# q, k, v projections with the weights stationary, and transposes back to token rows, in a hybrid decoder layer

## The chip, the cores and the metric

The kernel runs on one core of one Trainium2 chip. A core has a matrix engine (TensorE; the profile calls its matmuls PE and its weight loads PEld), a vector engine (VectorE, DVE), a scalar engine (ScalarE, ACT), a general one (GpSimd, POOL) and a queue engine that only starts transfers (SyncE, SP). The metric is the device time of one execution in microseconds, as the median of three runs.

## The reference, cut to what matters

One layer of a decoder runs for 1024 prompt tokens and 64 sample tokens, 1088 in all, of 1024 features, in float32. The part that matters here sits between the two feed-forward blocks:

```
h = rms(x)
[q | k | v | u | g_a | g_b] = h @ w_in      # q, k, v: 768 features each = 12 heads x 64
q = head_rmsnorm(q);  k = head_rmsnorm(k)   # mean of squares over the 64 features of a head
A = dilated sliding-window attention, 3 groups of 4 heads, (window, dilation) =
    (128, 1), (512, 4), (2048, 16)
B = causal pooling over u
x += (sigmoid(g_a) * (A @ w_attn_branch) + sigmoid(g_b) * (B @ w_pool_branch)) @ w_out
```

The normed k and the raw v of the last tokens are outputs too.

## The kernel before, in words

Every float32 product is made of three matmuls on a high and a low part (`mm3`, lines 252 to 259): high by high, high by low, low by high. The normed activations lie in SBUF as `h_hi` and `h_lo`, features on partitions, 8 blocks of 128 features by 1088 tokens. The tokens are cut into three chunks `CH` of 364, 362 and 362 columns (line 30).

`proj` (line 261) multiplies a 128-wide piece of a weight (stationary) by a chunk of tokens (moving): 24 matmuls, with 128 features on the partitions of the result. The feed-forward blocks, the pooling input u and the gates g_a and g_b go this way.

q, k and v go another way, in `qkv` (line 644), called for head group 2, then 1, then 0, each time for q, k and v ("kinds") of 256 features. For the dilated groups the prompt tokens are needed in another order: group 2 takes every eighth token into one tile of 128, group 1 every fourth. `permuted` (line 599) picks such a tile straight from `h_hi` and `h_lo`, with a step of 8 or 4 elements, as the stationary operand; the 256 columns of the weight move. The result has tokens on partitions. A ninth tile holds tokens 960 to 1087, of which only the last 64, the sample tokens, are used. Five units a kind (four of two tiles, one of the ninth) each fill one PSUM bank of the pool "a" (`psa`, four banks). For q and k the unit then goes through `qk_norm` (line 707): ScalarE squares it, VectorE sums over each head, makes the inverse root in eleven small steps and multiplies; for k GpSimd multiplies by the gain; TensorE transposes the rows back to features on partitions (line 737), and ScalarE copies them to `qT` or `kT`. For v a copy to `vs` is all.

The order of the work is written out by an `Interleaver` (line 72): a clock counts microseconds of TensorE work as the dense matmuls are emitted, and jobs (the head norms, attention of the group before, `sample_scores` with its loads every 2.7 us of that clock, the pooling) are let in when the clock reaches their due time. A scheduler of the language then orders each engine's instructions from that. Scores, transposes and values of attention use the other four PSUM banks, pool "b" (`psb`). After the last group come the eight gate projections; while they run, the second half of the sample attention and the combination of the groups are done, and the merge waits for both.

Of the kernel before, what the change touches and what calls it, by code (L numbers as in the profile page):

```python
# [29 lines left out]
CH = ((0, 364), (364, 362), (726, 362))  # L30
# [87 lines left out]
def body(ctx, tc, x_prompt, x_sample, c128, c512, c2048, state_pool, rel_bias_table,  # L118
# [27 lines left out]
    def tmp():  # L146
        return tmp_pool[0].tile([P, 364], F32, tag="tmp", name="tmp", bufs=8)
# [130 lines left out]
    def rsqrt(v, y, t):  # L278
        """y = v ** -0.5: exponent-halving seed, then three Newton steps."""
# [38 lines left out]
    def normed(xt, c, gi, dg):  # L318
        """h = x * gain * r for a chunk, r on the diagonal blocks of dg."""
# [100 lines left out]
    def biases():  # L420
        """The bias of every lag, in the order that the layouts of the score tiles read them."""
# [21 lines left out]
    for c, (c0, n) in enumerate(CH):  # L443
# [22 lines left out]
        dg = ip.tile([P, 364], F32, tag="dg", name="dg", bufs=2)[:, :n]  # L466
# [16 lines left out]
    # sample rows' biases: 128 cached positions, then the 64 new tokens  # L483
# [62 lines left out]
    def pooling():  # L546
# [22 lines left out]
        for gi in range(4):  # L569
# [22 lines left out]
            for c0, n in CH:  # L592
                o = psb()[:, :n]
                PE.matmul(o, wgr[:, gi, :], d[:, c0:c0 + n], start=True, stop=True)
                y = pp.tile([P, 364], F32, tag="y", name="y", bufs=2)[:, :n]
# [3 lines left out]
    def permuted(g, t):  # L599
        """AP picker over h tiles for the 128 tokens of permuted tile t of group g."""  # L600
        if t == 8:
            return lambda a, k: a[:, k, TP - NS:T]
        if g == 0:
            return lambda a, k: a[:, k, t * P:(t + 1) * P]
        if g == 1:
            c, hf = t // 2, t % 2
            return lambda a, k: a[:, k, c + 512 * hf:c + 512 * hf + 509:4]
        return lambda a, k: a[:, k, t:t + 1017:8]

    def token_rows(dst, g, t):  # L610
        """Rows of dst (indexed by token) that tile t of group g holds."""
# [7 lines left out]
    def reversed_rows(dst, g, t):  # L619
        """Rows of dst (indexed by the token counted from the end) of tile t's reversed tokens."""  # L620
# [7 lines left out]
    def store_kv(g, t, kind, tl):  # L628
        if t == 8:
            G.dma_start(out=kv_scr[kind, g], in_=tl[NS:P, :])  # L630
# [13 lines left out]
    def qkv(g, gp, follow):  # L644
        qT = gp.tile([P, 2, TP], F32, name="qT")
        kT = gp.tile([P, 2, TP], F32, name="kT")
        vs = [gp.tile([P, 256], F32, name=f"v{t}") for t in range(8)]
# [3 lines left out]
        for kind in range(3):  # L651
            c0 = kind * AW + g * 256
            w = taken()
            if kind < 2:
# [4 lines left out]
                if kind == 0:  # L659
                    V.tensor_scalar(out=gt, in0=gt, scalar1=0.125, scalar2=None, op0=ALU.mult)  # L660
            for u in range(5):
                if u == 1:
                    fetch(wi[:, c0 + AW:c0 + AW + 256] if kind < 2 else follow)
                tiles = (2 * u, 2 * u + 1) if u < 4 else (8,)
                nt = len(tiles)
# [6 lines left out]
                if kind == 2:  # L672
                    for i, t in enumerate(tiles):
                        if t < 8:
                            vt = vs[t]
                        else:
                            vt = qp.tile([P, 256], F32, tag="v8", name="v8", bufs=1)
                        S.activation(vt, o[:, i * 256:(i + 1) * 256], AF.Copy)
                        store_kv(g, t, 1, vt)
                    il.advance(0.325)  # L680
                    continue
                jobs.append(il.spawn(qk_norm(g, kind, tiles, o, gt, qT if kind == 0 else kT,
                                             qs if kind == 0 else ks)))
                il.advance(0.325)
# [12 lines left out]
        for job in jobs[:5]:  # L697
            il.finish(job)

# [5 lines left out]
        return qT, kT, vs, il.spawn(tail(), 6)  # L705

    def qk_norm(g, kind, tiles, o, gt, dst, dst8):
# [3 lines left out]
        sq = xq()  # L711
        S.activation(sq[:, :n], o[:, :n], AF.Square)
        st = qp.tile([P, 3, 8], F32, tag="st", name="st", bufs=3)
        v, y, t_ = st[:, 0, :nh], st[:, 1, :nh], st[:, 2, :nh]
# [4 lines left out]
        xn = xq()  # L719
        V.tensor_tensor(out=xn[:, :n].rearrange("p (h d) -> p h d", d=64),  # L720
                        in0=o[:, :n].rearrange("p (h d) -> p h d", d=64),
                        in1=y.unsqueeze(2).to_broadcast([P, nh, 64]), op=ALU.mult)
        xv = xn[:, :n].rearrange("p (t f) -> p t f", f=256)
        if kind == 1 or nt == 1:
            G.tensor_tensor(out=xv, in0=xv, in1=gt.unsqueeze(1).to_broadcast([P, nt, 256]),
                            op=ALU.mult)
        for i, t in enumerate(tiles):
            if kind == 1:
                store_kv(g, t, 0, xn[:, i * 256:(i + 1) * 256])
            elif t == 8:  # L730
                G.dma_start(out=q_scr[g], in_=xn[NS:P, 0:256])
                q_ready[g] = True
        yield 5.5
        tr = psb()
        for i in range(nt):
            for hp_ in range(2):
                PE.transpose(out=tr[:, (hp_ * nt + i) * P:(hp_ * nt + i + 1) * P],
                             in_=xn[:, i * 256 + hp_ * P:i * 256 + (hp_ + 1) * P],
                             identity=flip if kind == 0 and nt == 2 else ident)
# [7 lines left out]
        else:  # L747
            S.activation(dst8, tr[:, :256].rearrange("p (a x) -> p a x", a=2)[:, :, NS:], AF.Copy)

    def attention(g, qkvs):  # L750
# [47 lines left out]
        def values(t, kt, us, pts):  # L798
            o = psb()[:, :256]
            for h in range(4):  # L800
                for i, k in enumerate(kt):
                    PE.matmul(o[:, h * 64:(h + 1) * 64], pts[i][:, h * P:(h + 1) * P],  # L802
                              vs[k][:, h * 64:(h + 1) * 64], start=i == 0, stop=i == len(kt) - 1)
# [19 lines left out]
    def sample_scores():  # L823
        """Products of each sample query with its cached keys, keys on partitions."""
# [187 lines left out]
    ctx_a, ctx_b = ExitStack(), ExitStack()  # L1012
    ga_p = ctx_a.enter_context(tc.tile_pool(name="ga_p", bufs=1))
# [28 lines left out]
    def second_half():  # L1042
# [4 lines left out]
        ctx_a.close()  # L1047
        cp = cmctx.enter_context(tc.tile_pool(name="cmb", bufs=2))
# [5 lines left out]
    def merge_inputs():  # L1054
        """The pooled and attended branches, split for the products of the merge."""
        for c0, n in CH:
            for i in range(6):
                t = y_p.tile([P, 364], F32, tag="yl", name="yl", bufs=3)[:, :n]
# [55 lines left out]
    # merge, output projection  # L1114
# [121 lines left out]
```

## Time and profile before

| | |
|---|---|
| median of three runs | 2544.18 us (2540.89 to 2544.44) |
| span of the profiled execution, first to last instruction | 2539.3 us |
| the profiled execution's own time beside that | not given; the span is 4.9 us under the median |
| mean granted TensorE clock | 0.994 |
| PE busy / PEld busy / DVE busy / ACT busy / POOL busy | 2511.2 / 2468.5 / 1146.0 / 583.5 / 200.3 us |

The busy time of an engine is the time in which at least one of its instructions was under way. Matmuls overlap one another in the records, so what one of them costs is read from the distance between the starts of neighbours and not from the length of its record. The stages of q, k and v follow one another: group 2 from 878.5 to 1037.0 us, group 1 to 1199.6 us, group 0 to 1313.1 us, and then the gates to about 1566 us.

### The profile page before, as it was taken

The page shows a single profiled execution, that of the slowest core. Times are in us where ns is not written, and L with a number is a line of the kernel's source. Part 1 is how long each engine was busy: PE and PEld are TensorE (multiplying, and loading weights), DVE is VectorE, ACT ScalarE, POOL GpSimd, SP SyncE. Part 2 cuts the span into 40 slices and gives each one's busy share as a digit, 9 for nine tenths or more (in the row PEclk, how much of TensorE's full clock was granted, in tenths as well). Part 3 has the DMA queues.
Part 4 walks back from the last instruction along what each step waited for, and adds up shares of the span by engine and source line. Part 5 has one row for each costly group of instructions (what it writes and reads, how often), then busy time and mean ns, then how long its engine had stood idle before and what let it go on. Part 6 is the DMA issues. An engine that isn't in the chain of part 4 may idle for free. (4 is left out here: it accounts for less than half of the span.)

```text
span 2539.3 us, 36519 instructions
## 1 busy us (share of the span) xinstructions
PE 2511.2 (99%) x15192; PEld 2468.5 (97%) x15192; DVE 1146.0 (45%) x2451; ACT 583.5 (23%) x1233; POOL 200.3 (8%) x317
## 2 busy tenths in 40 slices
PE   7999999999999999999999999999999999999999
PEld 6999999999999999999989979999999999999998
DVE  6333343333336634255887723737333334433334
ACT  5211111111112312132334213214111111111111
POOL 4200000000001202012021211002000000000001
PEclk8999999999999999999999999999999999999999
DMA  4311221212221211235574685541122222221132
GB/s 140 103 58 42 83 83 66 83 47 70 83 83 64 69 34 70 84 122 161 170 236 141 205 288 181 176 177 34 50 83 83 75 76 83 77 73 67 42 116 71
DMA packets 153591, 257.24 MB, mean 101 GB/s; under 512 B 12581, under 2 KB 122853, under 8 KB 152641
## 3 DMA queue, kind: packets, MB, share of 16 engines
q1 hardware_dynamic: 141296, 224.26, 26.8%
q0 software_dynamic: 12128, 30.64, 3.6%
q8 instruction: 119, 1.95, 0.3%
q14 instruction: 48, 0.39, 0.0%
HBM read 225.99 MB, written 73.57 MB: 118 GB/s over the span
## 5 line engine op out<-in xcount | busy, mean ns | idle before, releaser
L257 PE MATMUL psa<-h_hi,wh 128*128 128x362 f32 (+1 forms) x2784 | 916.6, 330 | 2.4 <-ACT h_hi L328 2.2
L258 PE MATMUL psa<-h_lo,wh 128*128 128x362 f32 (+1 forms) x2784 | 915.0, 329 | 1.8 <-DVE h_lo L329 1.8
L259 PE MATMUL psa<-h_hi,wl 128*128 128x362 f32 (+1 forms) x2784 | 916.5, 329 | 0.0
L357 DVE SCALAR_TENSOR_TENSOR xt<-psb,xt 128x364 f32<-128x364 f32 (+1 forms) x528 | 279.7, 534 | 635.4 <-PE psb L259 635.1
L257 PEld LDWEIGHTS psa<-h_hi,wh 128*128 128x128 f32 x2784 | 525.4, 189 | 12.3 <-issue 7.2
L258 PEld LDWEIGHTS psa<-h_lo,wh 128*128 128x128 f32 x2784 | 527.0, 189 | 4.7 <-DVE h_lo L329 2.1
L259 PEld LDWEIGHTS psa<-h_hi,wl 128*128 128x128 f32 x2784 | 525.5, 189 | 1.4 <-issue 0.8
L257 PE MATMUL psb<-hh,dh 128*128 128x362 f32 (+1 forms) x1056 | 347.6, 329 | 0.0
L258 PE MATMUL psb<-hl,dh 128*128 128x362 f32 (+1 forms) x1056 | 346.7, 328 | 0.0
L259 PE MATMUL psb<-hh,dl 128*128 128x362 f32 (+1 forms) x1056 | 346.1, 328 | 0.0
L257 PE MATMUL psa<-wh,h_hi 128*128 128x256 f32 x648 | 231.2, 357 | 0.0
L258 PE MATMUL psa<-wl,h_hi 128*128 128x256 f32 x648 | 230.3, 355 | 0.0
L259 PE MATMUL psa<-wh,h_lo 128*128 128x256 f32 x648 | 229.6, 354 | 0.0
L213 DVE TENSOR_TENSOR wl<-wr,wh 128x1024 fp32r<-128x1024 f32 (+1 forms) x142 | 168.2, 1206 | 86.8 <-ACT wh L212 86.8
L257 PEld LDWEIGHTS psb<-hh,dh 128*128 128x128 f32 x1056 | 198.7, 188 | 0.2
L259 PEld LDWEIGHTS psb<-hh,dl 128*128 128x128 f32 x1056 | 198.8, 188 | 0.0
L258 PEld LDWEIGHTS psb<-hl,dh 128*128 128x128 f32 x1056 | 198.7, 188 | 0.1
L212 ACT ACTIVATE dh<-dr 128x256 fp32r<-128x256 f32 x176 | 72.2, 417 | 504.1 <-PE psb L258 494.9
L212 ACT ACTIVATE wh<-wr 128x1024 fp32r<-128x1024 f32 (+1 forms) x142 | 141.1, 1040 | 181.3 <-PE psa L258 163.5
L258 PEld LDWEIGHTS psa<-wl,h_hi 128*128 128x128 f32 x648 | 178.4, 275 | 1.6 <-issue 1.0
L257 PEld LDWEIGHTS psa<-wh,h_hi 128*128 128x128 f32 x648 | 178.2, 275 | 1.2 <-issue 0.3
L259 PEld LDWEIGHTS psa<-wh,h_lo 128*128 128x128 f32 x648 | 178.5, 275 | 0.5 <-issue 0.3
(225 smaller groups left out, 1913.2 us busy)
## 6 DMA issues: line engine op xcount, KB each, us to landing
wr<-in_ffn_w_up_dram SPq DMA_DIRECT2D x88, 512.0 KB, 4.0
out_dram<-in_cache_kv_w_dram SPq DMA_DIRECT2D x32, 1020.0 KB, 8.8
qb<-q_scr SPq DMA_DIRECT2D x96, 256.0 KB, 4.0
dr<-in_ffn_w_down_dram SPq DMA_DIRECT2D x44, 512.0 KB, 4.4
wr<-in_w_in_dram SPq DMA_DIRECT2D x38, 512.0 KB, 4.6
kt<-in_cache_kv_w_dram SPq DMA_DIRECT2D x64, 256.0 KB, 3.8
vt<-in_cache_kv_w_dram SPq DMA_DIRECT2D x26, 512.0 KB, 8.0
t<-t_scr SPq DMA_DIRECT2D x16, 544.0 KB, 5.2
```

Of the source, the lines that this page charges most:

```text
L212: S.activation(hi, src, AF.Copy)
L213: V.tensor_tensor(out=lo, in0=src, in1=hi.bitcast(F32), op=ALU.subtract)
L257: PE.matmul(out, lh, rh, start=i == 0, stop=False)
L258: PE.matmul(out, lh, rl, start=False, stop=False)
L259: PE.matmul(out, ll, rh, start=False, stop=i == n - 1)
L357: V.scalar_tensor_tensor(out=xd, in0=o, scalar=0.5, in1=xd, op0=ALU.mult, op1=ALU.add)
```

## The change

The chunks become 360, 360 and 368 columns, so that all their borders are multiples of 8, and the temporaries that hold a chunk grow to 368. q, k and v are projected by `proj`, as u and the gates are: weights stationary, features on the partitions, six calls a kind. ScalarE copies each result out of PSUM into a tile `raw` and permutes the tokens as it does (`permute`), reading PSUM with a step of 8 or 4 elements. `token_major` then transposes each token tile back to token rows on TensorE, into a bank of pool "b", and the head norm reads that bank as it read the projection's bank before. The five norm jobs of a kind are let in from 1.5 us of the clock after the kind's last projection, 2 us apart, instead of one after each unit. The eight value tiles become one. The ninth tile has the 64 sample tokens alone. GpSimd's scratch for transfer descriptors is set to 4096 bytes instead of its default. Comments are blanked.

```diff
-CH = ((0, 364), (364, 362), (726, 362))
+CH = ((0, 360), (360, 360), (720, 368))
...
-    def permuted(g, t):
-        if t == 8:
-            return lambda a, k: a[:, k, TP - NS:T]
         if g == 0:
-            return lambda a, k: a[:, k, t * P:(t + 1) * P]
-        if g == 1:
-            c, hf = t // 2, t % 2
-            return lambda a, k: a[:, k, c + 512 * hf:c + 512 * hf + 509:4]
-        return lambda a, k: a[:, k, t:t + 1017:8]
+    def permute(g, dst, o, c):
+        c0, n = CH[c]
+        m = min(n, TP - c0)
+        if g == 0:
+            S.activation(dst[:, c0:c0 + n], o, AF.Copy)
+            return
+        if g == 2:
+            S.activation(dst[:, :TP].rearrange("p (r i) -> p r i", r=8)[:, :, c0 // 8:(c0 + m) // 8],
+                         o[:, :m].rearrange("p (i r) -> p r i", r=8), AF.Copy)
+        else:
+            dv = dst[:, :TP].rearrange("p (r f i) -> p r f i", r=4, f=2)
+            for hf in range(2):
+                a, b = max(c0, 512 * hf), min(c0 + m, 512 * hf + 512)
+                if a < b:
+                    S.activation(dv[:, :, hf, (a - 512 * hf) // 4:(b - 512 * hf) // 4],
+                                 o[:, a - c0:b - c0].rearrange("p (i r) -> p r i", r=4), AF.Copy)
+        if m < n:
+            S.activation(dst[:, TP:], o[:, m:n], AF.Copy)
...
     def qkv(g, gp, follow):
+            raw = [rp.tile([P, T], F32, tag="raw", name="raw") for _ in range(2)]
...
+            for f in range(2):
+                for c in range(3):
+                    if f == 0 and c == 1:
+                        fetch(wi[:, c0 + AW:c0 + AW + 256] if kind < 2 else follow)
+                    o = proj(w, f, c, h_hi, h_lo)
+                    permute(g, raw[f], o, c)
+                    go()
             for u in range(5):
-                if u == 1:
-                    fetch(wi[:, c0 + AW:c0 + AW + 256] if kind < 2 else follow)
                 tiles = (2 * u, 2 * u + 1) if u < 4 else (8,)
-                o = psa()
-                for i, t in enumerate(tiles):
-                    pk = permuted(g, t)
-                    mm3(o[:, i * 256:(i + 1) * 256],
-                        [(pk(h_hi, k), pk(h_lo, k), w[0][:, k, :], w[1][:, k, :])
-                         for k in range(KD)], 0.325)
...
-                jobs.append(il.spawn(qk_norm(g, kind, tiles, o, gt, qT if kind == 0 else kT,
-                                             qs if kind == 0 else ks)))
-                il.advance(0.325)
+                jobs.append(il.spawn(
+                    values_of(g, tiles, raw, vs) if kind == 2 else
+                    qk_norm(g, kind, tiles, raw, gt, qT if kind == 0 else kT,
+                            qs if kind == 0 else ks), 1.5 + 2 * u))
...
+    def token_major(raw, tiles):
+        o = psb()
+        rows = P if len(tiles) == 2 else NS
+        for i, t in enumerate(tiles):
+            for a in range(2):
+                PE.transpose(out=o[:rows, i * 256 + a * P:i * 256 + (a + 1) * P],
+                             in_=raw[a][:, t * P:t * P + rows], identity=ident)
+        return o[:rows, :len(tiles) * 256]
...
+    rp = rctx.enter_context(tc.tile_pool(name="rp", bufs=3))
...
-    nc = bacc.Bacc("TRN2", target_bir_lowering=False, num_devices=1)
+    nc = bacc.Bacc("TRN2", target_bir_lowering=False, num_devices=1,
+                   dynamic_dma_scratch_size=4096)
```

## Rows read from the trace of the kernel before

**Rows 1.** The page's first part: busy us (share of the span) xinstructions.
```profile
PE 2511.2 (99%) x15192; PEld 2468.5 (97%) x15192; DVE 1146.0 (45%) x2451; ACT 583.5 (23%) x1233; POOL 200.3 (8%) x317
```

**Rows 2.** Windows by stage: length, busy us of each engine (count), clock, DMA share, GB/s.
```profile
878.50:1037.00 158.50, 158.50 (x712) 156.13 (x711) 54.93 (x174) 27.76 (x54) 27.16 (x43) 1.00 0.20 63
1037.00:1199.60 162.60, 162.60 (x836) 160.77 (x836) 83.33 (x235) 40.81 (x118) 20.96 (x29) 1.00 0.40 128
1199.60:1313.10 113.50, 111.29 (x925) 106.99 (x925) 91.10 (x243) 41.48 (x121) 17.47 (x24) 1.00 0.56 177
1313.10:1566.00 252.90, 248.20 (x1691) 224.19 (x1690) 131.87 (x260) 73.62 (x182) 40.27 (x69) 0.99 0.66 216
```

**Rows 3.** Timeline of PE in group 2: start us, length, instruction.
```profile
899.79 0.40 PE L257 MATMUL psa<-wh,h_hi 128*128 128x256 f32 x1
...
911.14 0.41 PE L259 MATMUL psa<-wh,h_lo 128*128 128x256 f32 x1
911.39 0.60 PE L737 MATMUL psb<-flip,xq 128*128 128x128 f32 x4
911.74 0.49 PE L257 MATMUL psa<-wh,h_hi 128*128 128x256 f32 x1
912.07 0.41 PE L258 MATMUL psa<-wl,h_hi 128*128 128x256 f32 x1
```

**Rows 4.** The same in group 1 and, from 1199.64, in group 0.
```profile
1188.43 0.40 PE L257 MATMUL psa<-wh,h_hi 128*128 128x256 f32 x1
...
1199.40 0.39 PE L259 MATMUL psa<-wh,h_lo 128*128 128x256 f32 x1
1199.64 0.28 PE L257 MATMUL psa<-wh,h_hi 128*128 128x256 f32 x1
...
1209.58 0.28 PE L259 MATMUL psa<-wh,h_lo 128*128 128x256 f32 x1
```

**Rows 5.** Timeline of PEld in group 2, at the border of the ninth tile.
```profile
1034.54 0.34 PEld L259 LDWEIGHTS psa<-wh,h_lo 128*128 128x128 f32 x1
1034.78 0.21 PEld L257 LDWEIGHTS psa<-wh,h_hi 128*128 128x128 f32 x1
1034.92 0.19 PEld L258 LDWEIGHTS psa<-wl,h_hi 128*128 128x128 f32 x1
...
1037.66 0.31 PEld L257 LDWEIGHTS psa<-wh,h_hi 128*128 128x128 f32 x1
```

**Rows 6.** Timeline of PE in the projection of u, weights stationary.
```profile
871.73 0.32 PE L257 MATMUL psa<-h_hi,wh 128*128 128x362 f32 x1
...
878.43 0.33 PE L259 MATMUL psa<-h_hi,wl 128*128 128x362 f32 x1
```

**Rows 7.** Groups by shape: busy us, mean ns | idle before; ACT and DVE copies from PSUM.
```profile
L1103 ACT ACTIVATE xq<-psa 128x362 f32<-128x362 f32 x32 | 14.9, 464 | 54.8 <-PE psa L259 50.1 <-issue 4.8
L1188 DVE COPY yo<-psa 128x256 f32<-128x256 f32 x8 | 3.4, 420 | 1.4 <-issue 0.8 <-PE psa L1181 0.6
```

**Rows 8.** The strided copies out of PSUM in the sample attention (tile pz).
```profile
L946 DVE COPY pz<-psb x1: 425/425/425, 1446.6 to 1446.6; 128x256 f32<-128x256 f32 x1
```

**Rows 9.** Timeline of the head norm of one q unit, ACT and DVE.
```profile
902.89 0.60 ACT L712 ACTIVATE xq<-psa 128x512 f32<-128x512 f32 x1 [7.38 <-PE psa L259]
903.52 0.69 DVE L715 TENSOR_REDUCE st<-xq 128x8 f32<-128x512 f32 x1 [4.08 <-ACT xq L712]
...
906.72 0.69 DVE L720 TENSOR_TENSOR xq<-psa,st 128x512 f32<-128x512 f32 x1
```

**Rows 10.** Groups of POOL from 878 to 1313 us: busy us, mean ns | idle before.
```profile
L725 POOL TENSOR_TENSOR xq<-xq,gt 128x512 f32<-128x512 f32 (+1 forms) x18 | 21.7, 1204 | 65.8 <-DVE xq L720 38.4 <-issue 16.6 <-PE psb L737 10.8
```

**Rows 11.** Groups of DVE in group 1's stage, 1037 to 1200 us.
```profile
L827 DVE TENSOR_TENSOR qb<-kt,qb 128x512 f32<-128x512 f32 x27 | 19.5, 722 | 6.6 <-DMA qb<-q_scr 6.6
L829 DVE TENSOR_REDUCE sc<-qb 128x8 f32<-128x512 f32 x27 | 18.4, 683 | 0.3
```

**Rows 12.** All products of the sample scores: duration ns min/median/max, first and last start.
```profile
L827 DVE TENSOR_TENSOR qb<-kt,qb x96: 670/684/1657, 1040.5 to 1427.5; 128x512 f32<-128x512 f32 x96
```

**Rows 13.** DMA issues: KB each, median us to landing.
```profile
qb<-q_scr SPq DMA_DIRECT2D x96, 256.0 KB, 4.0
x_scr<-xt POOLq DMA_DIRECT2D x2, 1448.0 KB, 7.3
```

More of the change, by code (lines that the diff above doesn't have):

```diff
@@ L146, in tmp @@
     def tmp():
-        return tmp_pool[0].tile([P, 364], F32, tag="tmp", name="tmp", bufs=8)
+        return tmp_pool[0].tile([P, 368], F32, tag="tmp", name="tmp", bufs=8)
     ident = const.tile([P, P], F32, name="ident")
@@ L465, in body @@
         rsqrt(st[:, 0, ts], st[:, 1, ts], st[:, 2, ts])
-        dg = ip.tile([P, 364], F32, tag="dg", name="dg", bufs=2)[:, :n]
+        dg = ip.tile([P, 368], F32, tag="dg", name="dg", bufs=2)[:, :n]
         t0 = c0
@@ L629, in store_kv @@
         if t == 8:
-            G.dma_start(out=kv_scr[kind, g], in_=tl[NS:P, :])
+            G.dma_start(out=kv_scr[kind, g], in_=tl[:NS, :])
             G.dma_start(out=kvs[g][:, WIN[g] - Q:WIN[g], kind * 256:(kind + 1) * 256],
@@ L646, in qkv @@
         kT = gp.tile([P, 2, TP], F32, name="kT")
-        vs = [gp.tile([P, 256], F32, name=f"v{t}") for t in range(8)]
+        vs = gp.tile([P, 8, 256], F32, name="vs")
         jobs = []
@@ L703, in tail, with values_of, qk_norm @@
             yield from new_scores()
-        return qT, kT, vs, il.spawn(tail(), 6)
-    def qk_norm(g, kind, tiles, o, gt, dst, dst8):
+        return qT, kT, vs, il.spawn(tail(), 11)
+    def token_major(raw, tiles):
[6 more added lines that the diff above has]
+        return o[:rows, :len(tiles) * 256]
+    def values_of(g, tiles, raw, vs):
+        o = token_major(raw, tiles)
+        il.clock += 0.22 * len(tiles)
+        if len(tiles) == 1:
+            vt = xq()[:, :256]
+            S.activation(vt[:NS], o, AF.Copy)
+            store_kv(g, 8, 1, vt)
+            return
+        S.activation(vs[:, tiles[0]:tiles[0] + 2, :], o.rearrange("p (t f) -> p t f", f=256), AF.Copy)
+        for t in tiles:
+            store_kv(g, t, 1, vs[:, t, :])
+        return
+        yield
+    def qk_norm(g, kind, tiles, raw, gt, dst, dst8):
         nt = len(tiles)
@@ L710, in qk_norm @@
         nh = nt * 4
-        sq = xq()
-        S.activation(sq[:, :n], o[:, :n], AF.Square)
+        o = token_major(raw, tiles)
+        rows = o.shape[0]
+        il.clock += 0.22 * nt
+        sq = xq()[:rows]
+        S.activation(sq[:, :n], o, AF.Square)
         st = qp.tile([P, 3, 8], F32, tag="st", name="st", bufs=3)
-        v, y, t_ = st[:, 0, :nh], st[:, 1, :nh], st[:, 2, :nh]
+        v, y, t_ = st[:rows, 0, :nh], st[:rows, 1, :nh], st[:rows, 2, :nh]
         V.tensor_reduce(out=v, in_=sq[:, :n].rearrange("p (h d) -> p h d", d=64), axis=AX.X,
@@ L718, in qk_norm @@
         rsqrt(v, y, t_)
-        xn = xq()
+        xn = xq()[:rows]
         V.tensor_tensor(out=xn[:, :n].rearrange("p (h d) -> p h d", d=64),
-                        in0=o[:, :n].rearrange("p (h d) -> p h d", d=64),
-                        in1=y.unsqueeze(2).to_broadcast([P, nh, 64]), op=ALU.mult)
+                        in0=o.rearrange("p (h d) -> p h d", d=64),
+                        in1=y.unsqueeze(2).to_broadcast([rows, nh, 64]), op=ALU.mult)
         xv = xn[:, :n].rearrange("p (t f) -> p t f", f=256)
         if kind == 1 or nt == 1:
-            G.tensor_tensor(out=xv, in0=xv, in1=gt.unsqueeze(1).to_broadcast([P, nt, 256]),
+            G.tensor_tensor(out=xv, in0=xv, in1=gt[:rows].unsqueeze(1).to_broadcast([rows, nt, 256]),
                             op=ALU.mult)
@@ L730, in qk_norm @@
             elif t == 8:
-                G.dma_start(out=q_scr[g], in_=xn[NS:P, 0:256])
+                G.dma_start(out=q_scr[g], in_=xn[:, 0:256])
                 q_ready[g] = True
@@ L736, in qk_norm @@
             for hp_ in range(2):
-                PE.transpose(out=tr[:, (hp_ * nt + i) * P:(hp_ * nt + i + 1) * P],
-                             in_=xn[:, i * 256 + hp_ * P:i * 256 + (hp_ + 1) * P],
-                             identity=flip if kind == 0 and nt == 2 else ident)
+                x = xn[:, i * 256 + hp_ * P:i * 256 + (hp_ + 1) * P]
+                if nt == 1:
+                    PE.transpose(out=tr[:, hp_ * NS:(hp_ + 1) * NS], in_=x,
+                                 identity=ident[:NS, :NS])
+                else:
+                    PE.transpose(out=tr[:, (hp_ * nt + i) * P:(hp_ * nt + i + 1) * P], in_=x,
+                                 identity=flip if kind == 0 else ident)
+        il.clock += 0.22 * nt
         if nt == 2 and kind == 0:
```

24 lines of the change are left out of this document (7 added, 17 removed).

## The prediction
> **What bounds the kernel now.** I read the page's busy times first. TensorE is busy 99% of the span and its weight loads 97%, with no other engine above 45% [rows 1], so whatever shortens TensorE's stream shortens the kernel until another engine or a transfer comes to be late. The busy share doesn't say what a matmul costs, so next come the windows by stage: groups 2, 1 and 0 take 158.5, 162.6 and 113.5 us, 434.6 us in all, at a granted clock of 1.00, with 2.2 us of idle PE, all of it in group 0 [rows 2]. The three issue the same dense matmuls, 1944 in all (3 groups, 3 kinds, 9 tiles, 24 each). The timeline tells why they differ. In group 2, 48 matmuls from 899.79 to 911.14 are 47 distances of 0.2415 us [rows 3]; in group 1, 47 distances from 1188.43 to 1199.40 are 0.2334; in group 0, 83 distances from 1199.64 to 1209.58 are 0.1198 [rows 4]. The moving operand is 256 contiguous columns in all of them; only the step of the stationary tile differs: 8, 4 and 1. The ninth tile, which is contiguous in every group, is the control: at its border, inside group 2, the weight load falls from 0.34 to 0.19 us and 24 loads take 2.88 us, 0.12 each [rows 5]. So groups 2 and 1 are bound by strided weight loads.
>
> **What the projections cost before.** A kind has 8 strided tiles of 24 matmuls and one contiguous. Group 2: 576 x 0.2415 + 72 x 0.1198 = 147.7 us. Group 1: 576 x 0.2334 + 72 x 0.1198 = 143.1. Group 0: 648 x 0.1198 = 77.6. Sum 368.4 us. The other 66.2 us of the stages are transposes, pooling products, attention of the group before and the idle time; they stay.
>
> **What they cost after.** Six calls of 24 matmuls a kind, 1296 in all, on 1088 / 3 = 362.7 columns on average. The same form, weights stationary and contiguous, ran in the projection of u: 42 matmuls of 362 columns, 41 distances from 871.73 to 878.43, 0.1634 us each [rows 6]; scaled to 362.7 columns 0.1637, so 212.2 us. The rows of the ninth tile that were computed twice are gone in this.
>
> **Transposes added.** Per kind 8 tiles x 2 and 2 for the sample rows, 162 in all. Four in group 2 lie between the matmuls that start at 911.14 and 912.07; less two distances of 0.24 that is 0.45 us for four, 0.112 each with the slower restart behind them [rows 3]. 162 x 0.112 = 18.1 us. The transposes back exist already. Net: 368.4 - 212.2 - 18.1 = 138.1 us off TensorE's stream. The chunks of 360 and 368 move the same columns everywhere else: nothing.
>
> **ScalarE's permuting copies.** About 63 of them, less the value copies that go. The nearest copy is 0.464 us for 362 columns [rows 7]; below I bound a strided one at that, above at twice. All but the last of a kind are hidden by the dense matmuls behind them (four banks in pool "a", 24 matmuls or 3.9 us each). The last one stands before the first transposes, which come 1.5 us of clock later, so it needs no wait at 0.5 us; at 0.9 us with a weight split ahead on ScalarE, 9 waits of at most 1 us. In group 1's window ScalarE goes from 40.8 us in 162.6 to some 52 in 96. I take 0 to 9 us and put 2 into the sum.
>
> That a step in PSUM is free, the trace shows for VectorE: 256 columns read with a step of 64 took 425 ns against 420 contiguous [rows 7, 8]. The Trainium skill (Advanced Engine Details and Errata, PSUM Cachelines) asks that every two consecutive PSUM elements be contiguous for best throughput, and `permute` reads with steps of 4 and 8. By the rule the copies are at their upper bound and the sum 7 us worse; by the row it stays. The skill's SBUF page (SBUF — State Buffer, Door 1) calls a step of up to 4 float32 free; by that group 1 would have run like group 0 and the gain would be 65 us smaller, which the 0.2334 contradicts.
>
> **Head norms, the one place where work is bunched.** The chain of a unit runs from 902.89 to 907.41, 4.5 us, of which VectorE holds 3.9 [rows 9]; k adds 1.2 us on GpSimd [rows 10]. Before, units came 5.2 us of clock apart; now five come 2 us apart behind a kind. Queued behind them on VectorE are the weight splits and the sample products, and each unit now holds a bank of pool "b" for some 6 us, which attention wants too. TensorE itself needs nothing from the chain but the transposes back: until then it has the next kind's dense matmuls, 3.9 us a call, about 23 us in all. The limit is VectorE's total. In group 1 it was busy 83.3 us of 162.6 [rows 2]; the stage shrinks to 162.6 - 143.1 + 70.7 + 6.0 = 96.2 us. The sample products (1.4 us a pair) follow the clock, which is as long as before and slightly more, so 27 pairs become some 29 [rows 11]: 86 us, plus some 4 us of gaps between the small steps. Group 0: 91.1 + 7 us in 113.5 - 77.6 + 70.7 + 6.0 = 112.6, less the idle time. Group 2, without sample products, 54.9 in 87.5. So VectorE is 94% full in group 1 and 87% in group 0. Below, nothing is lost; above, if every wait for a sample load (6.6 us in group 1 [rows 11]) and the bunching show, some 25 us. Group 0 ran at 80% before and lost 2.2 us [rows 2], the nearest row; I take 6.
>
> **Transfers.** Group 1 moved 128 GB/s at a share of 0.40 [rows 2], which is 0.68 in 96.2 us; the gates ran at 0.66 with 216 GB/s, so the queues have carried it. The next weights are fetched after one call of six instead of one unit of five, 18 us before use against a landing time near 5. The stores of k and v go out on POOL in the same number, later by up to a kind; nothing waits for them before the second half of the sample attention. The smaller descriptor scratch touches POOL's queue: if its 1448 KB spills blocked POOL for their 7.3 us [rows 13], only the last of three would have little cover; 0 to 7 us, and I take 0, since 24 matmuls of the u projection, four times over, stand before each norm's result.
>
> **Sum.** The span of 2539.3 lies 4.9 under the median of 2544.2, and I take that margin as fixed. 2539.3 - 138.1 + 2 + 6 = 2409.2 in span, 2414 us in time.
>
> **Rivals.** *VectorE becomes the bound in groups 1 and 0:* its queue holds back the transposes, pool "b" stays full and TensorE idles for the 25 us above: 2433 us. For it speaks the 94%; against it that the work can slide into group 2's end and the gates, where VectorE is half idle [rows 2].
>
> *The sample attention becomes late:* its 96 products span 1040.5 to 1427.5, 4.0 us each [rows 12], while the clock asks for 2.7. If loads and not the clock set that pace, they still need 387 us, and the second half 136 us more (1430 to 1566), 523 us from group 1's start; TensorE would have 96 + 113 + 253 = 462. The merge then waits 61 us: 2475 us. Against it: group 2's step of 0.24 where the clock counted 0.108 explains the pace, and a load lands in 4.0 us [rows 13].
>
> *Every chain lies bare:* the banks of pool "b" are so taken that TensorE stops at each unit until its norm is through. 12 pairs of q at 4.5 us, 12 of k at 5.7, 6 ninth tiles at 3.8 and 9 last copies at 1 us make 154 us, more than the 138 saved: 2560 us, slower. It turns slower once nine tenths of that price are paid, that is, if the next kind's dense matmuls cover almost nothing.
>
> *The change doesn't do what it says:* the slow weight load isn't the step's doing, or the strided copies stall pool "a" as much. The ninth tile in the same group speaks against it; half the gain would be left, 2475 us.
>
> **Chances.** Forecast 0.74 (own range 2400 to 2424), VectorE the bound 0.13, sample late 0.06, half the gain 0.04, chains bare 0.03. The range of 2398 to 2440 takes in the first two and leaves out 0.13; its low end is the sum with no stall and with the idle time of group 0 and some of the gates' 4.7 us [rows 2] gone. All but the last are faster by over 0.2%, the 5 us that a measurement of this kernel can tell: faster 0.96, same 0.01, slower 0.03.
>
> **What would show it.** PE distances of 0.163 us on 360 columns in all three stages, no PEld of 0.33 us left, stages near 88, 96 and 113 us; 162 more transposes at about 0.11; PE idle under 10 us from group 2 to the merge. Wrong it is if PE sits idle before the transposes on VectorE or ScalarE, if VectorE shows over 95% in group 1 with PE waiting, or if the gates' stage grows beyond 253 us.

## The result and the profile after

The changed kernel takes 2478.87 us (median of 4 runs, 2476.85 to 2484.49), the one before 2544.31 beside it: a ratio of 0.9751, 95% interval 0.9737 to 0.9764. So 65 us came of the 130 that the prediction has, and the time lies 39 us above the upper end of its range. The profiled run took 2478.45 us with a span of 2476.7. Its page, first part, answers to [rows 1]:

```profile
PE 2400.4 (97%) x14706; PEld 2344.0 (95%) x14706; DVE 1151.3 (46%) x2451; ACT 604.0 (24%) x1293; POOL 203.2 (8%) x317
```

TensorE now idles for 76.3 us of the span, 28.1 before. Windows by stage, the borders put where the dense matmuls of one group end and the next begin; columns and stages as in [rows 2] (groups 2, 1, 0, gates):

```profile
876.76:962.38 85.62, 85.62 (x517) 81.83 (x517) 42.89 (x126) 28.14 (x58) 13.29 (x22) 1.00 0.25 76
962.38:1056.89 94.51, 93.62 (x615) 89.71 (x615) 61.22 (x177) 40.97 (x120) 20.43 (x30) 1.00 0.51 160
1056.89:1205.03 148.14, 122.75 (x740) 112.44 (x739) 100.33 (x258) 49.52 (x137) 22.24 (x31) 0.86 0.54 169
1205.03:1507.84 302.81, 273.57 (x1830) 245.84 (x1830) 162.48 (x354) 88.14 (x225) 53.34 (x83) 0.93 0.61 197
```

Groups 2 and 1 are done in 85.6 and 94.5 us, as forecast (88 and 96). Group 0 takes 148.1 instead of 113 and the gates, counted here up to the first matmul of the merge, 302.8 instead of 253 (257.3 by that border before). From the merge on nothing changed: 968.9 us to the end in both. The clock of the third column from the right says that the two bad stages also ran part of the time at half speed.

The dense matmuls themselves are what was forecast. PE's timeline in group 2, answering to [rows 3, 4], and the groups of ScalarE's permuting copies by shape (busy us, mean ns | idle before), answering to [rows 7]:

```profile
890.73 0.33 PE L258 MATMUL psa<-h_lo,wh 128*128 128x360 f32 x1
...
896.95 0.33 PE L257 MATMUL psa<-h_hi,wh 128*128 128x360 f32 x1
```

```profile
L607 ACT ACTIVATE raw<-psa 128x360 f32<-128x360 f32 x12 | 5.6, 475 | 22.3 <-PE psa L259 16.0 <-PE psb L710 4.5 <-issue 1.7
L604 ACT ACTIVATE raw<-psa 128x360 f32<-128x360 f32 x12 | 5.4, 473 | 8.3 <-PE psa L259 7.2 <-PE psb L710 1.0
L614 ACT ACTIVATE raw<-psa 128x360 f32<-128x360 f32 x6 | 2.9, 487 | 3.9 <-PE psa L259 3.8
```

38 distances in 6.22 us are 0.1637 us each, the number of the sum. L607 reads PSUM with a step of 8, L614 with a step of 4, L604 contiguously: 475, 487 and 473 ns.

What was not forecast are the holes in TensorE. Its two longest sums of waits in the whole run (waited for: us in total, times, longest):

```profile
PE psb L766 <- POOL xq L749: 35.1, 6, 12.1
PE psb L817 <- ACT s L808: 6.3, 4, 2.5
```

L766 are the transposes of a normed unit back to columns, L749 is the k gain on GpSimd, the last step of the norm chain. One of the deepest holes lies at 1063 to 1093 us, at the k units of group 1 (a "unit" is a pair of token tiles, or the ninth, on its way through the head norm). First PE, start us, length, instruction, and in brackets the idle time before it:

```profile
1062.75 0.33 PE L259 MATMUL psa<-h_hi,wl 128*128 128x360 f32 x1
...
1074.36 3.62 PE L710 MATMUL psb<-ident,raw 128*128 128x128 f32 x16
1087.41 1.12 PE L766 MATMUL psb<-ident,xq 128*128 128x128 f32 x4 [9.43 <-POOL xq L749]
1089.21 0.64 PE L710 MATMUL psb<-ident,raw 128*64 128x128 f32 x2 [0.69 <-ACT kT L774]
1090.19 0.67 PE L257 MATMUL psa<-h_hi,wh 128*128 128x360 f32 x1 [0.35 <-ACT raw L614]
1090.66 0.50 PE L258 MATMUL psa<-h_lo,wh 128*128 128x360 f32 x1
...
1093.06 0.37 PE L257 MATMUL psa<-h_hi,wh 128*128 128x360 f32 x1
```

The last dense matmul is at 1062.75; then come only attention of group 2, the first transposes of four units (L710), a wait, the first unit's transposes back and, behind them, the first transposes of the fifth unit (128*64, at 1089.21). VectorE in the same stretch; L856 and L858 are a sample product and its sum, L739 and L744 the first and last step of a unit's norm:

```profile
1074.16 0.69 DVE L856 TENSOR_TENSOR qb<-kt,qb 128x512 f32<-128x512 f32 x1 [3.20 <-DMA qb<-q_scr]
...
1080.06 0.69 DVE L856 TENSOR_TENSOR qb<-kt,qb 128x512 f32<-128x512 f32 x1 [1.09 <-DMA qb<-q_scr]
1080.67 0.68 DVE L739 TENSOR_REDUCE st<-xq 128x8 f32<-128x512 f32 x1
...
1085.32 0.69 DVE L744 TENSOR_TENSOR xq<-psb,st 128x512 f32<-128x512 f32 x1
```

The first unit's square was ready at 1076.1; VectorE takes it up at 1080.67, behind products that wait for their loads. And ScalarE:

```profile
1075.46 0.60 ACT L736 ACTIVATE xq<-psb 128x512 f32<-128x512 f32 x1 [0.47 <-PE psb L710]
1076.36 0.60 ACT L736 ACTIVATE xq<-psb 128x512 f32<-128x512 f32 x1 [0.30 <-PE psb L710]
1088.56 0.60 ACT L774 ACTIVATE kT<-psb 128x512 f32<-128x512 f32 x1 [11.61 <-PE psb L766]
1089.06 0.59 ACT L736 ACTIVATE xq<-psb 128x512 f32<-128x512 f32 x1
1089.67 1.21 ACT L614 ACTIVATE raw<-psa 128x360 f32<-128x360 f32 x4
```

Two squares go at once, the third 12.7 us later, behind the first unit's transposes back. Behind it ScalarE empties the dense banks of pool "a" in a burst, and only then has TensorE dense work again. That burst also stands behind the fifth unit's transposes, and so it is in the whole run: a kind takes two of three `raw` tiles, so its second one is a tile of the kind before, which that kind's five units have to read first. All eight times the first copy into it (the last here at 1236.27) starts 0.3 to 0.9 us after the fifth unit's transposes of the kind before (there 1235.81), four times with ScalarE idle until then.

### The profile page after: what moved, and what is told of

It is laid out like the page before. It is cut to its first block, busy times and chain, and to the rows that moved or that the text cites. A ratio compares the mean times of both kernels' runs of the same rounds, so it can differ in the third digit from the quotient of the medians.

```text
span 2476.7 us, 35593 instructions
## 1 busy us (share of the span) xinstructions
PE 2400.4 (97%) x14706; PEld 2344.0 (95%) x14706; DVE 1151.3 (46%) x2451; ACT 604.0 (24%) x1293; POOL 203.2 (8%) x317
## 2 busy tenths in 40 slices
DMA packets 153586, 257.17 MB, mean 104 GB/s; under 512 B 12580, under 2 KB 122852, under 8 KB 152640
## 4 chain that ended last, share of the span: by engine, by line
PE 85%; issue 5%; DMA 4%; DVE 4%; POOL 1%; ACT 0%; SPq 0%; DVEq 0%; POOLq 0%
PE psa L258 21%; PE psa L257 20%; PE psa L259 20%; PE psb L258 7%; PE psb L257 7%; PE psb L259 7%; DMA qb<-q_scr 3%; DVE qb L856 1%; DVE sc L858 1%; DMA u_scr<-us 1%; PE psb L1017 1%; DMA wr<-in_ffn_w_up_dram 1%; PE psb L831 0%; POOL xq L749 0%; PE psa L1213 0%
## 5 line engine op out<-in xcount | busy, mean ns | idle before, releaser
L257 PE MATMUL psa<-h_hi,wh 128*128 128x360 f32 (+1 forms) x3216 | 1064.5, 331 | 4.5 <-ACT h_hi L328 2.0
L258 PE MATMUL psa<-h_lo,wh 128*128 128x360 f32 (+1 forms) x3216 | 1064.2, 331 | 1.9 <-DVE h_lo L329 1.9
L259 PE MATMUL psa<-h_hi,wl 128*128 128x360 f32 (+1 forms) x3216 | 1061.3, 330 | 0.0
L257 PEld LDWEIGHTS psa<-h_hi,wh 128*128 128x128 f32 x3216 | 609.4, 190 | 12.0 <-ACT h_hi L328 2.7
L258 PEld LDWEIGHTS psa<-h_lo,wh 128*128 128x128 f32 x3216 | 609.5, 190 | 6.4 <-issue 2.9
L259 PEld LDWEIGHTS psa<-h_hi,wl 128*128 128x128 f32 x3216 | 609.0, 189 | 6.4 <-issue 5.2
L357 DVE SCALAR_TENSOR_TENSOR xt<-psb,xt 128x360 f32<-128x360 f32 (+1 forms) x528 | 279.8, 533 | 624.5 <-PE psb L259 624.2
L257 PE MATMUL psb<-hh,dh 128*128 128x360 f32 (+1 forms) x1056 | 347.2, 329 | 0.0
L258 PE MATMUL psb<-hl,dh 128*128 128x360 f32 (+1 forms) x1056 | 346.8, 328 | 0.0
L259 PE MATMUL psb<-hh,dl 128*128 128x360 f32 (+1 forms) x1056 | 346.2, 328 | 0.0
L856 DVE TENSOR_TENSOR qb<-kt,qb 128x512 f32<-128x512 f32 x96 | 67.3, 702 | 43.9 <-DMA qb<-q_scr 43.8
```

Source lines behind the costliest of these rows:

```text
L257: PE.matmul(out, lh, rh, start=i == 0, stop=False)
L258: PE.matmul(out, lh, rl, start=False, stop=False)
L259: PE.matmul(out, ll, rh, start=False, stop=i == n - 1)
L357: V.scalar_tensor_tensor(out=xd, in0=o, scalar=0.5, in1=xd, op0=ALU.mult, op1=ALU.add)
L856: V.tensor_tensor(out=qb, in0=kt.to_broadcast([P, 2, 256]) if g == 0 else kt, in1=qb, op=ALU.mult))
```

## Experiments

Times are medians; one without an interval is a single time.

**Which work makes the holes.** Three variants: without the products, with products that wait for no load, and the kernel before without products as the control. The first and the third leave out the sample products and sums (the scores are zero); the second multiplies by one tile loaded once, so its sample scores have other values.

```
 no_products, before_no_products          resident
-keep_in_program_order(V.tensor_tensor(   -  load(kt, ...); load(qb, ...)
-    out=qb, in0=kt, in1=qb))             +  kt = kt0            # loaded once
-V.tensor_reduce(out=sc[g], in_=qb)       +  V.tensor_tensor(out=qb, in0=kt, in1=kt0)
```

> The changed kernel without the products of the sample queries with their cached keys (their two VectorE steps are left out and the scores set to zero; all loads stay). Theory, late norms: the products, pinned in VectorE's queue and waiting there for their loads, make the head norms late, the norms hold the four banks of pool b, the fifth unit of a kind then can't free the two raw tiles, ScalarE can't drain pool a, and TensorE stops. Then PE's idle time falls from 76 us to under 40 and the time to 2410 to 2435 us. Rival, ScalarE: the permuting copies themselves are what stops TensorE; then the time stays above 2465 us.

> The changed kernel with the same 96 pairs of product and sum on VectorE, but on a tile that is loaded once, so that none of them waits for a load (the loads of keys and queries are left out, and the scores are wrong). Theory, late norms by waiting loads: most of the loss goes, 2415 to 2445 us. Rival, VectorE simply has too much work in these stages: the time stays above 2460 us.

> The kernel before, without the 96 sample products and their sums on VectorE (the sample scores are zero, the loads stay). My theory, that the products hurt only since the change, because the head norms in VectorE's queue behind them now hold TensorE up: 2525 to 2543 us, at most 20 us below the 2544.3 of before, and so 114 us or so above the changed kernel without products (2421.1). The rival, that the products always cost some 58 us because VectorE's time counts in either kernel: 2480 to 2495 us.

Measured: 2421.14, 2440.12 and 2530.41 us. So the products cost 58 us in the changed kernel and 12 in the one before (2542.15 beside it). Of the 58, 39 go with the loads; how much of the 12 does was not run. (The resident form also moves less, 214.41 MB against 257.17. Attention's wait for its own stores, `us<-u_scr`, did not get shorter by it, 21.4 us against 17.4 between 960 and 1300 us, which speaks for the waits and not for the traffic.)

**The small edits.** On the kernel before: chunks of 360, 360, 368, temporaries of 368, the smaller scratch.

> The kernel before with only the small edits of the change: chunks of 360, 360 and 368 columns, temporaries of 368, the smaller DMA scratch; the projections stay as they were. My theory, that these are worth nothing: ratio 0.998 to 1.002, 2539 to 2547 us. The rival, that the even chunks themselves take part of what I credit to the projections: below 2535 us; or that they cost something that hides a part of the gain: above 2550 us.

2540.44 us, ratio 0.9992 (0.9983 to 1.0001): nothing, as forecast.

**What ends TensorE's cover: a bank, a raw tile, the group.** The fifth unit's bank from pool "a", a fourth raw tile (on top of resident products), and the last group projected in the old way to token rows.

```
 fifth_in_a:     o = psb() if len(tiles) == 2 else psa()
 resident_raw4:  rp = tile_pool(name="rp", bufs=4)
 g0_rows_first:  if g == 0: the five units by mm3 with h stationary, as before
```

> The changed kernel, with only the transposes of a kind's fifth unit (the sample rows) going to a bank of pool a instead of pool b, so that both raw tiles come free without waiting for the first unit's norm. Theory, banks of pool b hold the raw tiles: TensorE gains up to 10 us a kind where it stopped, 2440 to 2465 us. Rival, VectorE overloaded: the norms are as late as before and the transposes back stand in TensorE's queue all the same, 2472 to 2485 us.

> The products on a tile that is loaded once (as in the run before with resident products, 2440.1 us: no product waits for a load, their values are not the real ones), and four raw tiles instead of three in the space that this sets free. My theory, that TensorE's cover during the norms' chain ends with the raw tiles: 2425 to 2434 us, TensorE idle 6 to 15 us less than with three. The rival, that the cover ends with the four PSUM banks of the second pool, which the units wait for, and a fourth raw tile changes nothing: 2437 to 2443 us.

> The changed kernel with group 0 alone projected as before (tokens stationary, which are contiguous there, so 0.12 us a matmul), one norm after each unit. The sum says that group 0 gains nothing by the change (77.6 us before, 76.8 after). Theory, the bunched norms are the loss: the stage of group 0 goes from some 180 us back to 113 to 120, and the time to 2415 to 2435 us. Rival, the sample products are late by then whatever group 0 does, and the wait only moves into the gates' stage: 2455 to 2480 us.

2496.4, 2436.76 and 2467.99 us (ratio 0.9701, 0.9685 to 0.9718). The first missed and is slower; the second moves 3 us, less than runs of one kernel differ by; the third gives 11 us and no more, as its rival said: the idle time moves, to 1110 to 1150 and 1190 to 1210 us. By their times none of the three shows what ends the cover; by their traces the first two do. The last dense matmul ahead of the hole in resident and in resident_raw4, and the first one behind it in fifth_in_a:

```profile
1061.22 0.33 PE L259 MATMUL psa<-h_hi,wl 128*128 128x360 f32 x1
1076.46 0.33 PE L259 MATMUL psa<-h_hi,wl 128*128 128x360 f32 x1
1079.49 0.67 PE L257 MATMUL psa<-h_hi,wh 128*128 128x360 f32 x1 [0.35 <-ACT raw L614]
```

With a fourth raw tile the dense work goes on 15 us longer and comes back at about the same time (1083.72 against 1084.08 us), so the stretch without it shrinks from 22.9 to 7.3 us. With the fifth unit's bank in pool "a" its transposes come early, and the dense work is back 4 us after the other four units' first transposes, ahead of any transposes back: 20.2 us without it (from 1059.27 us), 27.4 in the changed kernel. Both lose again later what they gain here. In resident_raw4 the waits for the k gain grow from 13.4 to 23.3 us in all; in fifth_in_a TensorE is busy 145.9 us of 1100 to 1300 us, against 161.2 in the changed kernel.

**The order on VectorE.** The products unpinned, spaced wider, held back while a unit is in work, or moved to GpSimd.

```
 not_pinned:     - tc.keep_in_program_order(V.tensor_tensor(out=qb, ...))   + V.tensor_tensor(out=qb, ...)
 space33:        SPACE = 3.3          # 2.7
 gated:          while any(not j[1] for j in busy): yield 1      # before multiply; SPACE = 2.0
 pool_products:  G.tensor_tensor(out=qb, ...)
```

> The changed kernel, but the sample products are no longer pinned to the order of the program: the planner may put a head norm ahead of products that wait for their loads. My theory (norms stand late in VectorE's queue, behind products that wait for loads): 2430 to 2465 us, TensorE idle for 20 to 35 us less than the 76.3 us of after, holes shorter in groups 1 and 0. The rival, that the planner's own estimate of the loads puts the products ahead of the norms just the same, or that another wait takes over: 2470 to 2490 us, the holes as in after.

> The changed kernel with the sample steps 3.3 us of TensorE work apart instead of 2.7 (96 steps over 317 us of work instead of 259). My theory: fewer products between two norms, the backlog that waits for loads is smaller, 2455 to 2474 us, and TensorE's idle time falls by 5 to 20 us. The rival, that the products then run later into group 0 and the sample attention ends late: 2479 to 2500 us, with a new wait before the merge at the end of the gates.

> The changed kernel in which no sample product is issued while a q or k unit of the head norms is in work; in between a step goes out every 2.0 us of TensorE work instead of every 2.7. My theory: with no product ahead of a norm in VectorE's queue the holes of groups 1 and 0 go as they did without products; what remains to pay is a late sample attention. 2430 to 2465 us. The rival, that the products then pile up into the gates and the merge waits for the sample attention for as much as the holes cost: 2470 to 2520 us, with TensorE idle around the end of the gates.

> The changed kernel with the 96 sample products on GpSimd, the sums stay on VectorE. My theory (the norms are late because VectorE stands at products whose loads have not landed): a product that waits on GpSimd lets VectorE go on until the sum, which still waits for it; some 66 us of products leave VectorE. 2440 to 2465 us. The rival, that the wait only moves: the k norms' gain (L749) and the DMA issues on GpSimd stand behind the products instead, and the sums on VectorE wait as the products did: 2475 to 2510 us, TensorE's waits for L749 above the 35.1 us of after.

2527.65 (0.9938, 0.9923 to 0.9952), 2488.83 (0.9788, 0.9772 to 0.9804), 2483.04 (0.9768, 0.9751 to 0.9784) and 2477.11 us (0.9745, 0.9730 to 0.9759): four times my theory missed, and the first lies above its rival's range too. TensorE's waits of not_pinned:

```profile
PE psb L766 <- POOL xq L749: 56.6, 10, 20.1
PE psb L763 <- POOL xq L749: 10.7, 2, 7.8
```

Left alone, the planner makes the waits for the k gain 56.6 + 10.7 = 67.3 us where after has 35.1. So the pin had been a help, and that later norms go with a longer time fits; my guess of which way the planner would move them was wrong. In space33 the rival's new wait is there, at the merge:

```profile
PE psa L257 <- ACT y_hi L212: 7.7, 3, 6.6
```

gated tells nothing: between 1065 and 1095 us VectorE still had 12 products between the steps of the norms, so holding the emission back did not hold the queue's order. In pool_products the wait moved to VectorE's sums, here between 960 and 1300 us; TensorE's wait for the k gain fell to 17.5 us, which the rival had the other way:

```profile
DVE sc L858 <- POOL qb L856: 53.8, 27, 6.3
```

**The place of the transposes back, and the tiles of the norm.** A unit takes two of three `xq` tiles, one for the squares, one for the normed values, which it holds until its transposes back. So the square of the unit after next needs the tile that the first unit's transposes back still have to read. The edit gives the squares a tile of their own in the same space; the other one lets the transposes back in later.

```
 sq_own:   - sq = xq()[:rows]     # xq: bufs=3
           + sq = qp.tile([P, 512], F32, tag="sq", name="sq", bufs=1)[:rows]     # xq: bufs=2
 back10:   - yield 5.5            + yield 10            # ahead of the transposes back
```

> The changed kernel with the transposes back to columns (L766) let in 10 us of TensorE work after a unit's start instead of 5.5, and the squares in a tile of their own so that a unit's first step need not wait for the transposes back of the unit before the last. My theory: TensorE's queue holds more dense products of the next kind ahead of the transposes that are not ready, the holes shrink by some 4.5 us each, 2450 to 2470 us. The rival, that the third raw tile and the four PSUM banks end the cover anyhow, so that TensorE stops at the dense products or the units' transposes instead: 2472 to 2490 us.

> Only the half of the last edit that gives the squares a tile of their own; the transposes back stay at 5.5 us. If the place of the transposes back in TensorE's queue made the gain of 21.8 us of the run with both: 2470 to 2480 us, as after. If it was the tile (a unit's square no longer waits for the transposes back of the unit before the last): 2455 to 2462 us.

2456.64 us with both (0.9663, 0.9648 to 0.9677), 2447.36 with the tile alone (0.9631, 0.9616 to 0.9645), below both of the figures I had for it. The later place costs 9 us; the tile gives 31.5. The same k units of group 1 as above in sq_own, ScalarE's squares and copies, and TensorE from the first transposes back to its dense work:

```profile
1060.37 0.60 ACT L736 ACTIVATE sq<-psb 128x512 f32<-128x512 f32 x1
1064.13 0.60 ACT L736 ACTIVATE sq<-psb 128x512 f32<-128x512 f32 x1 [3.16 <-DVE st L739]
1065.54 0.60 ACT L736 ACTIVATE sq<-psb 128x512 f32<-128x512 f32 x1 [0.81 <-DVE st L285]
1066.95 0.60 ACT L736 ACTIVATE sq<-psb 128x512 f32<-128x512 f32 x1 [0.81 <-DVE st L285]
...
1072.86 0.66 ACT L614 ACTIVATE raw<-psa 128x360 f32<-128x360 f32 x2 [0.39 <-PE psb L710]
```

```profile
1071.18 0.66 PE L766 MATMUL psb<-ident,xq 128*128 128x128 f32 x4 [2.07 <-POOL xq L749]
1072.52 0.41 PE L710 MATMUL psb<-ident,raw 128*64 128x128 f32 x2 [0.69 <-ACT kT L774]
1073.38 0.43 PE L257 MATMUL psa<-h_hi,wh 128*128 128x360 f32 x1 [0.45 <-ACT raw L614]
```

Four squares in 6.6 us, and a first wait of 2.07 us in place of 9.43. The dense work still stops after the same call as in the changed kernel, here at 1068.78, and its way back is written out step by step in the brackets: transposes back, the copy to `kT` that gives a bank of pool "b" free, the fifth unit's transposes, the copies into `raw`, dense work. None of these four squares is late. The planner's order changed along with the tile, since it plans with it; how much of the 31.5 us is the wait for the tile and how much the better order is not told apart.

**One loss or two, and a better kernel.**

```
 resident_back10 = resident + sq_own + back10      pool_back10   = pool_products + sq_own + back10
 resident_sq     = resident + sq_own               back10_g0rows = g0_rows_first + sq_own + back10
                                                   sq_own_g0rows = g0_rows_first + sq_own
```

> Both edits (10 us to the transposes back, squares in their own tile) with the products on a tile that is loaded once. If the two causes are apart, the waits for loads (39 us) and the work of the products that TensorE's queue has no cover for (19 us): 2420 to 2430 us, near the 2421 without products. If the edits help only against the waits, so that the resident products leave them nothing: 2437 to 2442 us.

> Both edits, and the products on GpSimd. If the later transposes back also cover GpSimd's queue (the k gain behind the products there), 2440 to 2453 us, below the 2456.6 us of both edits alone. If the products on GpSimd only move the wait, as they did in the changed kernel: 2454 to 2470 us.

> Both edits, and the last group projected to token rows as in the kernel before. If the holes that the edits leave lie as much in group 0 as in group 1: 2440 to 2452 us. If group 0's dense work in rows costs more than its holes (the old form takes 0.12 us for 256 columns against 0.164 for 360): 2457 to 2475 us.

> The squares in a tile of their own, and the products on a tile that is loaded once. If the shared tiles and the waits for loads are one loss (a norm that waits holds its tiles, and the next units with it): 2432 to 2440 us, no more than 10 us below the 2447.4 us of the own tile alone, and close to the 2440.1 us of the resident products alone. If they are two losses that add up: 2440.1 - 31 = 2405 to 2415 us.

> The squares in a tile of their own, and the last group projected to token rows as in the kernel before. TensorE's longest holes with the own tile alone lie at 1200 to 1220 us, in group 0. If rows there take the holes away: 2432 to 2443 us. If the old form's dense work in group 0 costs as much as the holes: 2444 to 2455 us.

2435.82, 2466.77 (0.9705, 0.9690 to 0.9720), 2450.42 (0.9643, 0.9627 to 0.9659), 2415.22 and 2437.12 us (0.9586, 0.9570 to 0.9602). resident_back10 lies between its two figures and decides nothing by itself, but beside resident_sq it says that the later place costs 20.6 us there; GpSimd is no help here either. resident_sq decides: 2415.2 us, 63.7 below the changed kernel. Its page's first part and its windows by stage:

```profile
PE 2380.6 (99%) x14706; PEld 2330.7 (97%) x14706; DVE 1134.0 (47%) x2451; ACT 605.5 (25%) x1293; POOL 206.7 (9%) x317
```

```profile
876.14:962.83 86.69, 86.69 (x528) 82.89 (x528) 48.01 (x171) 31.37 (x65) 19.17 (x29) 1.00 0.26 84
962.83:1061.81 98.98, 98.98 (x681) 95.32 (x681) 63.09 (x171) 46.59 (x139) 20.15 (x29) 1.00 0.23 69
1061.81:1172.32 110.51, 107.95 (x699) 101.74 (x699) 85.83 (x233) 46.23 (x130) 21.89 (x28) 0.97 0.18 56
1172.32:1444.62 272.30, 262.03 (x1794) 236.79 (x1794) 152.82 (x344) 84.24 (x207) 51.80 (x81) 0.98 0.49 159
```

All of VectorE's work is still there, and group 0 takes 110.5 us, the gates 272.3. The fastest kernel that computes everything is sq_own_g0rows, 41.8 us below the changed kernel: own tile for the squares, and the contiguous group in token rows as before.

## Why the prediction was half right

- *Dense work, 138.1 us.* Right: 0.1637 us a matmul, groups 2 and 1 in 85.6 and 94.5 us; in resident_sq, with few holes, PE is busy 130.6 us less than before (2380.6 against 2511.2). That the change takes the slow weight loads away is settled by that; that the step made them slow rests on the ninth tile [rows 5].
- *The permuting copies, 2 us.* Right. The Trainium skill's rule (Advanced Engine Details and Errata, PSUM Cachelines), weighed in the prediction, would have them dearer; 475 ns with a step of 8 and 487 with a step of 4 against 473 without one, ScalarE hardly shows it.
- *The small edits, nothing.* Right: 0.9983 to 1.0001.
- *Sample attention late.* Did not come: the last product starts at 1360.2 us and no wait of TensorE stands at the merge. All products of the changed kernel, duration ns min/median/max, first and last start, answering to [rows 12]:

```profile
L856 DVE TENSOR_TENSOR qb<-kt,qb x96: 664/685/1776, 964.8 to 1360.2; 128x512 f32<-128x512 f32 x96
```

  In space33, with wider spacing, waits of 7.7 us do stand there, so it may have been near.
- *VectorE becomes the bound, 2433 us.* Not by its total: resident_sq runs all of its work in 2415.2 us. The 86 us in group 1's 96 did not come about either, since work slid on into the next stage: VectorE has 61.2 of 94.5 us there.
- *The other rivals.* Two of them, sample attention late and half the gain, stood at 2475 us, 4 us from the measured time, and neither's mechanism came about: that is luck. *Every chain lies bare* was given 0.03 and came nearest in kind, since TensorE does stop at units whose norm is not through; but it idles 55.5 us from group 2 to the merge, not the 154 us of every chain.
- *The step that failed:* "TensorE itself needs nothing from the chain but the transposes back: until then it has the next kind's dense matmuls, 3.9 us a call, about 23 us in all. The limit is VectorE's total." With it fell the 6 us put down for VectorE's stalls, which were some 64 us too few. What was weighed were the two engines' totals, and not the order of their queues, nor the tiles and banks that a unit holds. The cover itself is about as long as forecast: in the hole above seven calls, 27 us, stand between the end of the k matmuls and the stop. But the dense work needs more from the chain than the transposes back. Its results fill the four banks of pool "a" until the five units' first transposes have set a raw tile free, and the fifth unit's transposes wait for a bank of pool "b" that comes free only behind the first unit's whole norm and transposes back (1087.41, 1089.21, 1089.67 and 1090.19 us in the rows of the changed kernel above; the same order with releasers in sq_own). Before, a unit's norm came every 11 us or more, as its own projection did; the first two squares of the same k units of group 1 in the kernel before (the next follow at 1142.21 and 1153.71):

```profile
1107.65 0.59 ACT L712 ACTIVATE xq<-psa 128x512 f32<-128x512 f32 x1
1118.48 0.59 ACT L712 ACTIVATE xq<-psa 128x512 f32<-128x512 f32 x1
```

After, five come at once at a kind's end. Two things hold them up then, each taken away by a run of its own. They share three tiles, so that the third unit waits for the first one's transposes back (the run that parts them changes the planner's order as well); and VectorE's queue has sample products ahead of them that wait for loads of 3.9 us. Tiles first: 31.5 us (2478.9 to 2447.4), then loads 32.2 (to 2415.2); in the other order 38.8 (2440.1) and 24.9. Either way 63.7 us, where the forecast was off by 64.9. That the two agree to 1 us is partly luck: the kernel before waited for such loads as well, so some of the loads' part, at most the 12 us that all products cost there, is not the change's. The shared tiles cost little while VectorE is prompt: without products the kernel takes 2421.1 us with the tiles still shared, 5.9 above resident_sq (single times both). TensorE pays twice, once in idle time and once in the clock: from group 2's start to the merge it idles 42.7 us more than in resident_sq (55.5 against 12.8), and is busy 19.9 us longer (575.6 against 555.7) with the same instructions.

What ends the cover in the hole at 1063 us is thus the raw tile and, through the fifth unit, the bank of pool "b"; a fourth tile and a bank of pool "a" each made this hole shorter, though not the kernel much faster. ScalarE's late squares are not it: in sq_own the squares are early and the dense work stops at the same call. Two things stay open: why the first transposes of the k units come only at 1074.36, behind attention of group 2 that itself waits, which is the first 12 us of this hole; and what loses again, later in the run, the gain of fifth_in_a and resident_raw4.

## To carry to other kernels

When a change turns work that came evenly into bursts, the totals of the engines say little: count the tiles that one unit of the burst holds, and see what its last reader waits for, before counting busy time; then ask what the dense work behind it needs from those same tiles and banks. Look also at what stands ahead of the burst in each engine's queue and whether that waits for a transfer; a wait that cost a few us in a slack stage is paid in full in a tight one. Where a stage has no strided operand, leave it as it was: the old form in the contiguous group, with the tiles apart, is the fastest version here.

## What the runs showed of the hardware

The holes cost more than they are long. In the hole above the granted clock is 0.50, the lower level (1.2 GHz), from 1070 to 1090 us, after TensorE's dense work had stopped at 1062.75; the dense matmuls that follow go 0.30 us apart from 1090.66 to 1093.06 and come back to 0.164 only behind that:

```profile
1070.00:1080.00 10.00, 7.29 (x33) 6.27 (x32) 5.06 (x8) 3.83 (x13) 1.09 (x2) 0.50 0.94 284
1080.00:1090.00 10.00, 1.75 (x6) 0.90 (x6) 9.02 (x32) 1.42 (x3) 1.84 (x2) 0.50 0.57 186
1090.00:1100.00 10.00, 9.59 (x50) 9.26 (x51) 7.73 (x22) 2.93 (x9) 3.82 (x3) 0.84 0.39 121
```

These are windows of 10 us, columns as in [rows 2]. And a step of 8 elements in PSUM costs ScalarE 2 ns in 475 for 360 columns, and a step of 4 costs 14 in 487.
